# Masked softmax with given lengths: which engine loads the first four batches, and in which order

## The chip, the core and the metric

The kernel runs on one core of one Trainium2 chip. The metric is the device time of one execution in microseconds; three runs of the kernel before gave a median of 156.31 us (156.04 to 156.49). Five engines take part: SyncE (SP) issues DMAs, GpSimd (POOL) issues DMAs and does small set-up work, VectorE (DVE) and ScalarE (ACT) compute, and TensorE (PE) does two tiny matmuls. All DMAs, whoever issues them, are moved by the core's 16 DMA engines.

## The reference

The input x has 16 batches of 8 heads of 256 rows of 256 float32; each batch has a length between 128 and 255.

```python
for b in range(batch):
    length = lengths[b]
    masked = x[b, :, :, :length].copy()
    masked = masked - np.max(masked, axis=-1, keepdims=True)
    exp_masked = np.exp(masked)
    result[b, :, :, :length] = exp_masked / np.sum(exp_masked, axis=-1, keepdims=True)
```

Columns from the length on are zero in the result. The lengths of the draw used are 188, 233, 229, 243, 195, 252, 165, 210, 222, 180, 209, 157, 159, 199, 214, 248.

## The kernel before

One batch is 2048 rows: 128 partitions with 16 rows each, 2 MB. The tile xt holds 8 slots of one batch; batch n lives in slot n % 8 from its load to its store, and every step works in place.

For each batch, in order, there are these steps:

- Load. SyncE issues batches 0 to 3 whole (lines 128 to 132, batch 0 as two halves), all at the start, on its own DMA queue (q1). GpSimd issues batches 4 to 15 on another queue (q0), in a loop of six turns with two loads each (lines 177 to 184). A loaded row is only as wide as the batch needs: `pick` (line 147) compares the length with the widths 160, 168, up to 240, and 256, by nested branches, and issues the DMA with the first width that holds the length.
- Mask. VectorE's clip (line 221) takes, over columns 128 to 255, the smaller of x and a number that is very large inside the length and very negative outside it. Columns that were not loaded hold old finite data or zeros, and are masked too.
- Exponential. ScalarE (line 328) works row by row of each partition, 16 instructions a batch, and adds up the row sums.
- Divide. VectorE takes the reciprocal of the sums (line 242) and multiplies each half batch by it (line 245).
- Store. SyncE issues the stores on the same queue as its loads (lines 134 to 143), whole or cut into halves and quarters by `parts`.

VectorE's order is written out: for batch 0 and from batch 4 on, the first half's divide, then the next batch's mask, then the second half's divide; for batches 1 to 3 the next batch's mask comes first.

The order between engines is set by semaphores. Stores start only after the third half batch has been exponentiated (line 134), and a batch's stores wait until those of the batch two before have landed (line 140). s_st counts landed stores, one semaphore for even batches and one for odd ones; each is started at 64 by a small memset (line 170). Before the loop, GpSimd zeroes columns 160 to 255 of slots 4 to 7, which have never held a whole batch (line 173; four memsets), after it has waited for VectorE's set-up (line 171). Then it waits for the lengths, for these four fills, and for batch 2 to land (s_ld[3], line 176). In the loop a load waits, from the second turn on, until the load two batches before it has landed (s_sw, line 182) and until the batch that last used the slot is stored (s_st, line 183).

At the end, VectorE checks sums and lengths, and a rarely used second path (from line 290 on) would do everything again with the row maximum subtracted.

Of the kernel before, what the change touches and what calls it, by code (L numbers as in the profile page):

```python
# [9 lines left out]
F32 = mybir.dt.float32  # L10
# [7 lines left out]
POOL = mybir.EngineType.Pool  # L18
# [3 lines left out]
def kernel(  # L22
# [6 lines left out]
    nc = tc.nc  # L29
    P = nc.NUM_PARTITIONS  # L30

    batch, heads, seq_q, seq_k = x.shape
# [6 lines left out]
    x_f = x.rearrange("b h q k -> b (h q) k").rearrange("b (p t) k -> b p t k", p=P)  # L39
    out_f = out.rearrange("b h q k -> b (h q) k").rearrange("b (p t) k -> b p t k", p=P)  # L40

    slots = 8
    ahead = 4
    assert slots - ahead == 4 and batch % slots == 0

    widths = list(range(160, 248, 8))
    low = widths[0]
# [3 lines left out]
    def parts(b):  # L51


        if b == 0:
            cuts = [0, nt]
        elif b < 8:
            cuts = [0, half, half + quarter, nt]
        elif b < 13 or b == batch - 1:
            cuts = [0, half, nt]
        else:  # L60
            cuts = [0, nt]
        return [slice(i, j) for i, j in zip(cuts, cuts[1:])]

    pool = ctx.enter_context(tc.tile_pool(name="all", bufs=1))
    psum = ctx.enter_context(tc.tile_pool(name="psum", bufs=1, space=bass.MemoryType.PSUM))
    xt = pool.tile([P, slots, nt, seq_k], F32, name="xt")
    word64 = pool.tile([1, batch], mybir.dt.int64, name="word64")
    word = word64.bitcast(I32)
# [3 lines left out]
    len_s = pool.tile([P, batch], F32, name="len_s")  # L72
# [2 lines left out]
    row_sum = pool.tile([P, batch, nt], F32, name="row_sum")  # L75
    inv_sum = pool.tile([P, batch, nt], F32, name="inv_sum")
    warm = pool.tile([P, 1], F32, name="warm")
    seed = pool.tile([1, 2], F32, name="seed")

    sum_low, sum_high = 1.0e-15, 1.0e30  # L80
    ones_c = pool.tile([P, 1], BF16, name="ones_c")
# [10 lines left out]
    s_st = [sem("s_st0"), sem("s_st1")]  # L92
    with tc.tile_critical(no_gpsimd_drain=True):  # L93
# [4 lines left out]
        s_ld = [sem(f"s_ld{k}") for k in range(ahead + 1)]  # L98

        s_sw = [sem("s_sw0"), sem("s_sw1")]  # L100

        s_iota = sem("s_iota")
        s_fill = sem("s_fill")
# [14 lines left out]
        def length(engine, at):  # L118

            return nc.values_load(  # L120
                at,
                engines=[engine],
                skip_runtime_bounds_check_because="compared with constants, never an address",
            )
# [2 lines left out]
        nc.scalar.dma_start(out=word64, in_=lengths[None, :]).then_inc(s_word, 16)  # L127
        for h in range(2):
            s = slice(h * half, (h + 1) * half)
            nc.sync.dma_start(out=xt[:, 0, s], in_=x_f[0, :, s]).then_inc(s_ld[h], 16)  # L130
        for b in range(1, ahead):
            nc.sync.dma_start(out=xt[:, b], in_=x_f[b]).then_inc(s_ld[b + 1], 16)  # L132

        nc.sync.wait_ge(s_exp, 3)
        for b in range(batch):
            s_b = s_st[b % 2]
            for s in parts(b):
                nc.sync.wait_ge(s_out, 2 * b + (s.stop - 1) // half + 1)
                if b >= 2 and s.start == 0:
                    nc.sync.wait_ge(s_b, 64 * (b // 2 + 1))  # L140
                nc.sync.dma_start(
                    out=out_f[b, :, s, :], in_=xt[:, b % slots, s, :]
                ).then_inc(s_b, 16 * ((s.stop - s.start) // quarter))


# [1 line left out]
        def pick(v, n, slot, par, ws):  # L147

            if len(ws) == 1:
                w = ws[0]  # L150
                nc.gpsimd.dma_start(  # L151
                    out=xt[:, slot, :, :w], in_=x_n[:, n, :, :w]
                ).then_inc(s_sw[par], 16)
                return
            m = (len(ws) - 1) // 2
            with nc.gpsimd.If(v <= ws[m]):  # L156
                pick(v, n, slot, par, ws[: m + 1])
            with nc.gpsimd.Else():
                pick(v, n, slot, par, ws[m + 1 :])
# [6 lines left out]
        ).then_inc(s_iota, 1)  # L166
        nc.gpsimd.memset(ones, 1.0).then_inc(s_ones, 1)  # L167
        nc.gpsimd.memset(ones_c, 1.0).then_inc(s_ones, 1)
        for par in range(2):
            nc.gpsimd.memset(seed[:, par : par + 1], 0.0).then_inc(s_st[par], 64)  # L170
        nc.gpsimd.wait_ge(s_v, 2)
        for b in range(ahead, slots):
            nc.gpsimd.memset(xt[:, b, :, low:], 0.0).then_inc(s_fill, 1)  # L173
        nc.gpsimd.wait_ge(s_word, 16)
        nc.gpsimd.wait_ge(s_fill, slots - ahead)
        nc.gpsimd.wait_ge(s_ld[ahead - 1], 16)
        with nc.Fori(0, (batch - ahead) // 2, 1, engines=[POOL]) as q:
            for par in range(2):
                n = 2 * q + (ahead + par)
                v_len = length(POOL, word[0:1, bass.ds(2 * n, 1)])  # L180
                with nc.gpsimd.If(q >= 1):  # L181
                    nc.gpsimd.wait_ge(s_sw[par], 16 * q)
                    nc.gpsimd.wait_ge(s_st[par], 64 * q)
                pick(v_len, bass.ds(n, 1), bass.ds(n % slots, 1), par, widths + [seq_k])


        nc.tensor.wait_ge(s_ones, 2)
# [8 lines left out]
        def step(ins):  # L196
# [8 lines left out]
                out=down, in0=iota_i, scalar1=0.5, scalar2=-big, op0=ALU.add, op1=ALU.mult  # L205
# [7 lines left out]
                out=len_s, in0=len_f, scalar1=big, scalar2=None, op0=ALU.mult  # L213
# [4 lines left out]
        def clip(b, s, lo, hi):  # L218

            t = xt[:, b % slots, s, lo:hi]  # L220
            return nc.vector.scalar_tensor_tensor(  # L221
                out=t,
                in0=down[:, None, lo:hi].to_broadcast([P, s.stop - s.start, hi - lo]),
                scalar=len_s[:, b : b + 1],
                in1=t,
                op0=ALU.add,
                op1=ALU.min,
            )

        def mask(b, s):  # L230
            if b == 0:
                nc.vector.wait_ge(s_ld[s.start // half], 16)
            elif b < ahead:
                nc.vector.wait_ge(s_ld[b + 1], 16)
            else:
                nc.vector.wait_ge(s_sw[b % 2], 16 * ((b - ahead) // 2 + 1))
            clip(b, s, mid, seq_k).then_inc(s_min, 1)

        def divide(b, h):
            s = slice(h * half, (h + 1) * half)  # L240
            nc.vector.wait_ge(s_exp, 2 * b + h + 1)
            step(nc.vector.reciprocal(out=inv_sum[:, b, s], in_=row_sum[:, b, s]))  # L242
            nc.vector.wait_ge(s_v, v)
            t = xt[:, b % slots, s, :]
            nc.vector.tensor_tensor(  # L245
                out=t,
                in0=t,
                in1=inv_sum[:, b, s, None].to_broadcast([P, half, seq_k]),
                op=ALU.mult,
            ).then_inc(s_out, 1)  # L250

        mask(0, slice(0, half))
        mask(0, slice(half, nt))
        for b in range(batch):


            first = b == 0 or b >= ahead
            if first:
                divide(b, 0)
            if b + 1 < batch:  # L260
                mask(b + 1, slice(0, nt))
            if not first:
                divide(b, 0)
            divide(b, 1)
# [14 lines left out]
        for k, (_, _, edge, op) in enumerate(checks):  # L279
            nc.vector.tensor_scalar(  # L280
                out=bad[:, k : k + 1],
# [13 lines left out]
        with nc.vector.Else():  # L295
            with nc.Fori(0, batch, 1, engines=[DVE]) as i:
                nc.vector.wait_ge(g_ld, 16 * i + 16)
                nc.vector.scalar_tensor_tensor(
                    out=g_t,
                    in0=down[:, None, :].to_broadcast([P, nt, seq_k]),  # L300
                    scalar=len_s[:, bass.ds(i, 1)],
# [6 lines left out]
                    out=neg_max, in_=g_t, op=ALU.max, axis=AX, negate=True  # L308
# [5 lines left out]
                    out=g_t,  # L314
# [24 lines left out]
        a_redo = length(ACT, redo_bits[0:1, 0:1])  # L339
        with nc.scalar.If(a_redo >= 1):  # L340
            for par in range(2):
                nc.scalar.wait_ge(s_st[par], 64 * (batch // 2 + 1))
            with nc.Fori(0, batch, 1, engines=[ACT]) as i:
                nc.scalar.dma_start(out=g_t, in_=x_g[:, bass.ds(i, 1)]).then_inc(g_ld, 16)
                nc.scalar.wait_ge(g_v, 3 * i + 2)
                with nc.Fori(0, nt, 1, engines=[ACT]) as t:
                    e = g_t[:, bass.ds(t, 1), :]
                    nc.scalar.activation(
                        out=e,
                        in_=e,  # L350
                        func=EXP,
                        bias=neg_max[:, bass.ds(t, 1)],
                        accum_out=sum_g[:, bass.ds(t, 1)],
                    ).then_inc(g_exp, 1)
                nc.scalar.wait_ge(g_out, i + 1)
                nc.scalar.dma_start(out=o_g[:, bass.ds(i, 1)], in_=g_t).then_inc(g_st, 16)
                nc.scalar.wait_ge(g_st, 16 * i + 16)


    with tc.tile_critical(no_gpsimd_drain=True):  # L360
        for par in range(2):
            nc.sync.wait_ge(s_st[par], 64 * (batch // 2 + 1))


# [28 lines left out]
```

## Time and profile before

| | |
|---|---|
| median of 3 runs | 156.31 us (156.04 to 156.49) |
| the profiled execution | 156.38 us |
| its span, first to last instruction | 154.8 us |
| VectorE busy, ScalarE busy | 116.8 us, 105.2 us |
| GpSimd busy | 19.1 us |
| DMA moved | 62.09 MB, 401 GB/s over the span |
| read from HBM, written to HBM | 28.51 MB, 33.55 MB |
| SyncE's three whole loads: issue to landing (median) | 16.0 us |
| first load by GpSimd issued at | 20.80 us |
| first store issued at | 19.62 us |

Times inside the execution are microseconds from the start of the span. A row of the profile's views names the source line, the engine and the operation, with what it writes and what it reads; "POOLq" and "SPq" are the instruction queues of GpSimd and SyncE. The DMA share of a stretch is the mean busy share of the 16 DMA engines in it. Packets that overlap in one engine can bring it a little above 1.

### The profile page before, as it was taken

Reading aid. Unit: us, or ns where it says so; the run is one execution under the profiler, and the core shown is the slowest. Engines: PE = TensorE matmul, PEld = TensorE weight load, DVE = VectorE, ACT = ScalarE, POOL = GpSimd, SP = SyncE. Lnnn points to the kernel's source line nnn. Section 1 sums busy time; section 2 is a strip of 40 time slices with the busy share of each in tenths; the row PEclk is TensorE's granted clock in tenths of the full one; section 3 lists DMA queues with packets and bytes.
Section 4 is the critical chain, followed back from the end, with each engine's and each line's share of the span. In section 5 each row is a group of like instructions: output and inputs, shape, how many; then the busy total and the mean of one; then the engine's idle time right before and its main releaser. Section 6 shows DMA issues by size and latency. Waiting matters only on the chain.

```text
span 154.8 us, 1298 instructions
## 1 busy us (share of the span) xinstructions
PE 0.3 (0%) x2; PEld 0.2 (0%) x2; DVE 116.8 (75%) x91; ACT 105.2 (68%) x514; POOL 19.1 (12%) x26
## 2 busy tenths in 40 slices
PE   0000000000000000000000000000000000000000
PEld 0000000000000000000000000000000000000000
DVE  1349999954999696969799796969696556986800
ACT  3096799991792959597796959595959709779000
POOL 4910031000220200202020020202010000000000
DMA  4999999999999999999999999999999999999992
GB/s 112 424 443 432 436 364 406 403 414 450 407 402 389 415 414 418 414 414 413 400 421 410 415 408 406 416 415 419 418 423 412 418 455 409 426 455 419 421 421 91
DMA packets 9989, 62.09 MB, mean 401 GB/s; under 512 B 850, under 2 KB 946, under 8 KB 6274
## 3 DMA queue, kind: packets, MB, share of 16 engines
q1 hardware_dynamic: 5904, 41.95, 65.7%
q0 software_dynamic: 4080, 20.12, 32.1%
q14 instruction: 3, 0.02, 0.0%
q10 hardware_dynamic: 2, 0.00, 0.0%
HBM read 28.51 MB, written 33.55 MB: 401 GB/s over the span
## 4 chain that ended last, share of the span: by engine, by line
DMA 73%; DVE 7%; issue 6%; ACT 4%; POOLq 2%; ACTq 1%; SPq 1%; PE 0%
DMA xt<-in_x_dram 73%; ACT xt L328 4%; DVE xt L221 3%; DVE xt L245 3%; ACTq L328 1%; POOLq L156 1%; POOLq L151 1%; SPq L130 1%; DVE ends L277 0%; POOLq L120 0%; DVE inv_sum L242 0%; SPq L132 0%; DVE bad L280 0%; POOLq L181 0%; ACTq L334 0%
## 5 line engine op out<-in xcount | busy, mean ns | idle before, releaser
L328 ACT ACTIVATE xt<-xt (+1 forms) x256 | 102.4, 402 | 36.1 <-DVE xt L221 36.1
L245 DVE TENSOR_TENSOR xt<-xt,inv_sum 128x2048 f32<-128x2048 f32 x32 | 73.3, 2292 | 1.1
L328 ACT ACTIVATION_READ_ACCUMULATOR xt<-xt (+1 forms) x256 | 48.0, 187 | 0.0
L221 DVE SCALAR_TENSOR_TENSOR xt<-down,len_s,xt 128x2048 f32<-128x2048 f32 (+1 forms) x17 | 37.8, 2222 | 12.1 <-DMA xt<-in_x_dram 11.9
L151 POOL DMA_DIRECT2D xt<-in_x_dram x12 | 12.8, 1066 | 94.5 <-DMA out_dram<-xt 61.1
L242 DVE RECIPROCAL inv_sum<-row_sum 128x8 f32<-128x8 f32 x32 | 6.3, 198 | 14.3 <-ACT xt L328 14.3
L173 POOL MEMSET xt<- 128x1536 f32 x4 | 5.3, 1393 | 1.1 <-DVE len_s L212 1.1
L321 ACT ACT_TABLE_LOAD x1 | 1.3, 1283 | 1.6 <-SPq L93 1.6
L204 DVE TENSOR_SCALAR down<-iota_i 128x256 f32<-128x256 int32 x1 | 0.3, 300 | 1.6 <-POOL iota_i L164 1.6
L277 DVE TENSOR_REDUCE ends<-row_sum 128x1 f32<-128x256 f32 x2 | 0.7, 408 | 0.0
L191 PE MATMUL count<-bad,ones_c 128*1 128x3 bf16 x1 | 0.2, 165 | 143.8 <-DVE bad L280 143.8
L209 DVE CAST len_b<-word 1x16 bf16<-1x16 int32 x1 | 0.2, 163 | 0.4 <-DMA word<-in_lengths_dram 0.4
L212 DVE TENSOR_SCALAR len_s<-len_f 128x16 f32<-128x16 f32 x1 | 0.2, 175 | 0.3 <-PE len_f L189 0.3
L164 POOL IOTA iota_i<- 128x256 int32 x1 | 0.3, 332 | 0.6 <-SPq L93 0.6
L288 DVE TENSOR_REDUCE redo<-count 1x1 f32<-1x3 f32 x1 | 0.1, 149 | 0.3 <-PE count L191 0.3
L280 DVE TENSOR_SCALAR bad<-ends 128x1 bf16<-128x1 f32 x3 | 0.3, 149 | 0.0
L170 POOL MEMSET seed<- 1x1 f32 x2 | 0.2, 226 | 0.0
L191 PEld LDWEIGHTS count<-bad,ones_c 128*1 128x1 bf16 x1 | 0.1, 79 | 143.9 <-DVE bad L280 143.9
L321 ACT ACTIVATE warm<-const-float32-0.0 128x1 f32<-128x1 f32 x1 | 0.2, 203 | 0.0
L167 POOL MEMSET ones<- 1x128 bf16 x1 | 0.2, 197 | 0.0
L189 PE MATMUL len_f<-len_b,ones 1*128 1x16 bf16 x1 | 0.2, 166 | 2.6 <-DVE len_b L209 2.6
L277 DVE TENSOR_REDUCE ends<-len_s 128x1 f32<-128x16 f32 x1 | 0.2, 157 | 0.0
(7 smaller groups left out, 0.6 us busy)
## 6 DMA issues: line engine op xcount, KB each, us to landing
out_dram<-xt SPq DMA_DIRECT2D x19, 1024.0 KB
out_dram<-xt SPq DMA_DIRECT2D x14, 512.0 KB
xt<-in_x_dram SPq DMA_DIRECT2D x3, 2048.0 KB, 16.0
out_dram<-xt SPq DMA_DIRECT2D x3, 2048.0 KB
xt<-in_x_dram POOLq DMA_DIRECT2D x3, 1728.0 KB, 16.4
xt<-in_x_dram POOLq DMA_DIRECT2D x2, 2048.0 KB, 18.5
xt<-in_x_dram POOLq DMA_DIRECT2D x2, 1600.0 KB, 16.4
xt<-in_x_dram POOLq DMA_DIRECT2D x2, 1280.0 KB, 14.5
```

Source lines behind the costliest of these rows:

```text
L130: nc.sync.dma_start(out=xt[:, 0, s], in_=x_f[0, :, s]).then_inc(s_ld[h], 16)
L151: nc.gpsimd.dma_start(out=xt[:, slot, :, :w], in_=x_n[:, n, :, :w]).then_inc(s_sw[par], 16)
L156: with nc.gpsimd.If(v <= ws[m]):
L164: nc.gpsimd.iota(iota_i, pattern=[[1, seq_k]], base=0, channel_multiplier=0).then_inc(s_iota, 1)
L173: nc.gpsimd.memset(xt[:, b, :, low:], 0.0).then_inc(s_fill, 1)
L191: nc.tensor.matmul(count, lhsT=ones_c, rhs=bad, start=True, stop=True).then_inc(s_count, 1)
L221: return nc.vector.scalar_tensor_tensor(out=t, in0=down[:, None, lo:hi].to_broadcast([P, s.stop - s.start, hi - lo]), scalar=len_s[:, b : ...
L242: step(nc.vector.reciprocal(out=inv_sum[:, b, s], in_=row_sum[:, b, s]))
L245: nc.vector.tensor_tensor(out=t, in0=t, in1=inv_sum[:, b, s, None].to_broadcast([P, half, seq_k]), op=ALU.mult,).then_inc(s_out, 1)
L277: step(nc.vector.tensor_reduce(out=ends[:, k : k + 1], in_=values, op=op, axis=AX))
L321: nc.scalar.activation(out=warm, in_=nc.const_aps.tensor(0.0, (P, 1), F32), func=EXP)
L328: ins = nc.scalar.activation(out=e, in_=e, func=EXP, accum_out=sum_h[:, i, j])
```

## The change

The order of work is no longer the order of the batches. A position is mapped to a batch by `batch_of`: positions 0, 1 and 2 are batches 1, 2 and 3, position 3 is batch 0, and from 4 on they agree. SyncE loads positions 0 to 2 whole. GpSimd loads positions 3 to 15 by their length, in a loop of seven turns whose last turn has one load. Its first load (batch 0, into slot 3) is issued after one fill and the lengths, with no wait for a landing. The other four fills, and the wait for position 2's landing, stand in the first turn, between the first load and the second. The semaphores of even and odd positions change places in the loop, and the one of the odd positions is started at 128.

```diff
-    ahead = 4
+    ahead = 3
+    def batch_of(pos):
+        return pos + 1 if pos < ahead else 0 if pos == ahead else pos
...
-            nc.sync.dma_start(out=xt[:, b], in_=x_f[b]).then_inc(s_ld[b + 1], 16)
+            nc.sync.dma_start(out=xt[:, b], in_=x_f[batch_of(b)]).then_inc(s_ld[b + 1], 16)
...
-                    nc.sync.wait_ge(s_b, 64 * (b // 2 + 1))
+                    nc.sync.wait_ge(s_b, 64 * (b // 2 + 1 + b % 2))
...
-        for par in range(2):
-            nc.gpsimd.memset(seed[:, par : par + 1], 0.0).then_inc(s_st[par], 64)
+        for k, par in enumerate((0, 1, 1)):
+            nc.gpsimd.memset(seed[:, k : k + 1], 0.0).then_inc(s_st[par], 64)
+        def fill(slot):
+            nc.gpsimd.memset(xt[:, slot, :, low:], 0.0).then_inc(s_fill, 1)
         nc.gpsimd.wait_ge(s_v, 2)
-        for b in range(ahead, slots):
-            nc.gpsimd.memset(xt[:, b, :, low:], 0.0).then_inc(s_fill, 1)
+        fill(ahead)
         nc.gpsimd.wait_ge(s_word, 16)
-        nc.gpsimd.wait_ge(s_fill, slots - ahead)
-        nc.gpsimd.wait_ge(s_ld[ahead - 1], 16)
-        with nc.Fori(0, (batch - ahead) // 2, 1, engines=[POOL]) as q:
-            for par in range(2):
-                n = 2 * q + (ahead + par)
-                v_len = length(POOL, word[0:1, bass.ds(2 * n, 1)])
-                with nc.gpsimd.If(q >= 1):
-                    nc.gpsimd.wait_ge(s_sw[par], 16 * q)
-                    nc.gpsimd.wait_ge(s_st[par], 64 * q)
-                pick(v_len, bass.ds(n, 1), bass.ds(n % slots, 1), par, widths + [seq_k])
+        nc.gpsimd.wait_ge(s_fill, 1)
+        turns = (batch - ahead + 1) // 2
+        with nc.Fori(0, turns, 1, engines=[POOL]) as q:
+            b = 2 * q + (q + 7) // 8 * ahead
+            v_len = length(POOL, word[0:1, bass.ds(2 * b, 1)])
+            with nc.gpsimd.If(q >= 1):
+                nc.gpsimd.wait_ge(s_sw[0], 16 * q)
+                nc.gpsimd.wait_ge(s_st[1], 64 * q)
+            pick(v_len, bass.ds(b, 1), bass.ds((2 * q + ahead) % slots, 1), 0, widths + [seq_k])
+            with nc.gpsimd.If(q < turns - 1):
+                b = nc.s_assert_within(2 * q + (ahead + 1), ...)
+                v_len = length(POOL, word[0:1, bass.ds(2 * b, 1)])
+                with nc.gpsimd.If(q >= 1):
+                    nc.gpsimd.wait_ge(s_sw[1], 16 * q)
+                    nc.gpsimd.wait_ge(s_st[0], 64 * q)
+                with nc.gpsimd.Else():
+                    for slot in range(ahead + 1, slots):
+                        fill(slot)
+                    nc.gpsimd.wait_ge(s_fill, slots - ahead)
+                    nc.gpsimd.wait_ge(s_ld[ahead], 16)
+                pick(v_len, bass.ds(b, 1), bass.ds(b % slots, 1), 1, widths + [seq_k])
...
-            first = b == 0 or b >= ahead
+            first = b == 0 or b > ahead
```

The remaining lines of the diff write batch_of(b) where VectorE picks a batch's length and where SyncE addresses the output, and carry the new counts to the last waits. VectorE's order over positions stays as it was over batches.

More of the change, by code (lines that the diff above doesn't have):

```diff
@@ L42 @@
     slots = 8
-    ahead = 4
-    assert slots - ahead == 4 and batch % slots == 0
+    ahead = 3
+    assert ahead == 3 and slots == 8 and batch == 16
+    def batch_of(pos):
+        return pos + 1 if pos < ahead else 0 if pos == ahead else pos
     widths = list(range(160, 248, 8))
@@ L77 @@
     warm = pool.tile([P, 1], F32, name="warm")
-    seed = pool.tile([1, 2], F32, name="seed")
+    seed = pool.tile([1, 3], F32, name="seed")
     sum_low, sum_high = 1.0e-15, 1.0e30
@@ L129 @@
             s = slice(h * half, (h + 1) * half)
-            nc.sync.dma_start(out=xt[:, 0, s], in_=x_f[0, :, s]).then_inc(s_ld[h], 16)
+            nc.sync.dma_start(out=xt[:, 0, s], in_=x_f[batch_of(0), :, s]).then_inc(s_ld[h], 16)
         for b in range(1, ahead):
-            nc.sync.dma_start(out=xt[:, b], in_=x_f[b]).then_inc(s_ld[b + 1], 16)
+            nc.sync.dma_start(out=xt[:, b], in_=x_f[batch_of(b)]).then_inc(s_ld[b + 1], 16)
         nc.sync.wait_ge(s_exp, 3)
@@ L139 @@
                 if b >= 2 and s.start == 0:
-                    nc.sync.wait_ge(s_b, 64 * (b // 2 + 1))
+                    nc.sync.wait_ge(s_b, 64 * (b // 2 + 1 + b % 2))
                 nc.sync.dma_start(
-                    out=out_f[b, :, s, :], in_=xt[:, b % slots, s, :]
+                    out=out_f[batch_of(b), :, s, :], in_=xt[:, b % slots, s, :]
                 ).then_inc(s_b, 16 * ((s.stop - s.start) // quarter))
@@ new lines @@
+        turns = (batch - ahead + 1) // 2
[7 more added lines that the diff above has]
+            with nc.gpsimd.If(q < turns - 1):
+                b = nc.s_assert_within(
+                    2 * q + (ahead + 1),
+                    ahead + 1,
+                    batch - 2,
+                    skip_runtime_bounds_check_because="q < turns - 1",
+                )
+                v_len = length(POOL, word[0:1, bass.ds(2 * b, 1)])
+                with nc.gpsimd.If(q >= 1):
+                    nc.gpsimd.wait_ge(s_sw[1], 16 * q)
[6 more added lines that the diff above has]
+                pick(v_len, bass.ds(b, 1), bass.ds(b % slots, 1), 1, widths + [seq_k])
@@ L223, in clip @@
                 in0=down[:, None, lo:hi].to_broadcast([P, s.stop - s.start, hi - lo]),
-                scalar=len_s[:, b : b + 1],
+                scalar=len_s[:, batch_of(b) : batch_of(b) + 1],
                 in1=t,
@@ L235, in mask @@
             else:
-                nc.vector.wait_ge(s_sw[b % 2], 16 * ((b - ahead) // 2 + 1))
+                nc.vector.wait_ge(s_sw[(b - ahead) % 2], 16 * ((b - ahead) // 2 + 1))
             clip(b, s, mid, seq_k).then_inc(s_min, 1)
@@ L341 @@
             for par in range(2):
-                nc.scalar.wait_ge(s_st[par], 64 * (batch // 2 + 1))
+                nc.scalar.wait_ge(s_st[par], 64 * (batch // 2 + 1 + par))
             with nc.Fori(0, batch, 1, engines=[ACT]) as i:
@@ L361 @@
         for par in range(2):
-            nc.sync.wait_ge(s_st[par], 64 * (batch // 2 + 1))
+            nc.sync.wait_ge(s_st[par], 64 * (batch // 2 + 1 + par))
 _INS = ['x', 'lengths']
```

## The prediction

> **What bounds the kernel now.** I read the page's busy times first, then its DMA queues, then the same by stretches of the span.
>
> ```profile
> PE 0.3 (0%) x2; PEld 0.2 (0%) x2; DVE 116.8 (75%) x91; ACT 105.2 (68%) x514; POOL 19.1 (12%) x26
> ...
> q1 hardware_dynamic: 5904, 41.95, 65.7%
> q0 software_dynamic: 4080, 20.12, 32.1%
> ```
>
> No compute engine is above 75%. The two queues' packets took 65.7 + 32.1 = 97.8% of the 16 DMA engines' span, 151.4 of 154.8 us. q1 is SyncE's queue (whole loads, then every store), q0 GpSimd's (loads by length). The stretches (columns: stretch, length, busy time of PE, PEld, DVE, ACT, POOL, clock, DMA share, GB/s) show no hole:
>
> ```profile
> 2.00:18.00 16.00, 0.17 (x1) 0.10 (x1) 9.69 (x9) 9.34 (x43) 5.34 (x4) 1.00 0.99 409
> 18.00:20.50 2.50, 0.00 (x0) 0.00 (x0) 2.40 (x2) 2.50 (x13) 0.00 (x0) 1.00 1.01 433
> 20.50:23.70 3.20, 0.00 (x0) 0.00 (x0) 3.13 (x5) 3.20 (x17) 1.30 (x1) 1.00 1.02 348
> ...
> 42.00:131.00 89.00, 0.00 (x0) 0.00 (x0) 73.90 (x51) 65.58 (x325) 9.78 (x9) 1.00 1.02 414
> 131.00:151.50 20.50, 0.17 (x1) 0.08 (x1) 13.31 (x16) 10.01 (x50) 0.00 (x0) 1.00 1.00 426
> ```
>
> The DMA share (next to last) is 1.0 from 2 us to the end. So the time is the first packet (2.15), plus the DMA engines' work, plus 1.7 us from the last landing (153.05 in the trace's landing records) to the end of the span. A byte less is time less, if no hole opens. SyncE's queue has the same reading:
>
> ```profile
> SPq L140 <- DMA out_dram<-xt: 95.3, 14, 9.3
> SPq L138 <- DVE xt L245: 14.6, 1, 14.6
> SPq L141 <- DVE xt L245: 11.4, 8, 3.3
> ```
>
> It waits 95.3 us for older stores to land and only 11.4 us for results: finished batches queue for the DMA.
>
> **The change, part by part.** I call position p the p-th batch worked on. Now p0 to p3 are batches 0 to 3, whole, through q1. After, p0 to p2 are batches 1 to 3, whole, and p3 is batch 0 through q0. Its length in the given draw is 188, so 192 of 256 columns are read.
>
> *Bytes.* A whole batch is 8 packets of 16384 B per DMA engine; their duration in the trace is 611 ns, so 4.89 us. A narrow batch is 128 rows per engine. Rows of 184 columns went six to a packet at 178 ns (29.7 each), rows of 200 six at 190.4 ns (31.7 each). Between them, 30.7 ns for 192: 128 x 30.7 = 3.93 us. Removed: **0.96 us** of every engine's work. Loads of p4 to p15 and all stores are unchanged.
>
> *When p3's packets start.* GpSimd's timeline now:
>
> ```profile
> 3.05 5.34 POOL L173 MEMSET xt<- 128x1536 f32 x4 [1.10 <-DVE len_s L212]
> 20.80 1.30 POOL L151 DMA_DIRECT2D xt<-in_x_dram  x1 [12.41 <-issue]
> 23.96 0.56 POOL L151 DMA_DIRECT2D xt<-in_x_dram  x1 [1.86 <-issue]
> ```
>
> After, one fill (1.39 us) ends at 4.44, and the wait for batch 2's landing no longer stands ahead of the first load. From that wait's end to the load took 18.57 to 20.80 = 2.23 us; with some 0.2 for the added register steps, the load issues at 6.9. Its first packet follows late: 20.80 to 26.22 now, 5.4 us (4.7 for a later load that met an empty q0). So p3 starts at **12.3**. The other four fills (5.6 us) come behind it on GpSimd, end before 18 even if they start at 12.3, and only p4's load waits on them.
>
> *What that does to q1.* Where both queues are full, the packet records alternate one for one whatever the size: in 1 us near 34 us, 47 packets of 4800 B on q0 beside 44 of 4096 on q1; near 37 us, 22 of 16384 beside 24 of 4096. At 12.3, q1 has 0.9 us of p1 (now landed at 13.21) and the 8 packets of p2 left: 9.5 packets, each followed by one of p3 at 184 ns. p1 lands at 13.5, p2 at 18.07 + 1.75 = **19.8**.
>
> *The hand-over to stores.* The first store is issued 6.4 us after p1 lands (13.21 to 19.62), so at 19.9; an issue takes 1.0 us to its first packet (1.13 to 2.15), so 20.9. From 19.8 to 20.9 q0 works alone: p3 has 12 of its 22 packets left, 2.2 us. No row shows a narrow load alone. The nearest, a whole load on q0 beside few stores (36 to 42 us), ran at 437 GB/s; I take 0, and if narrow packets alone ran at half rate, +0.55. Work then continues to 22.1 + 4.9 (store of p0) = 27.0. The next store needs p2: 18.07 to its issue at 23.39 is 5.3, plus 1.0: 19.8 + 6.3 = 26.1, before 27.0. p4's load, issued on p2's landing, took 18.07 to 26.22 = 8.15; so at most 28.0, and stores cover until then. No hole, with 0.9 us in hand.
>
> *A start-up loss.* From 20.5 to 23.7 p3's packets were stretched (up to 1.3 us instead of 0.61; the 348 GB/s above). Against the usual durations that is 0.7 us, right when GpSimd's first load and the first store are issued; otherwise only the very first loads show it. I take it as paid once as now. Bounds: gone, -0.7; paid twice, +0.7.
>
> *The added load on q0.* The last of the 16 completion writes came 0.06 us after the 15th at the first whole load, 0.42 at 96 us, 0.82 at the end: one engine falls behind, 0.76 us over ten narrow loads. One more: +**0.08**. The Trainium skill ("DMA: Bandwidth & Descriptors", Latency and other measured facts) tells of two engines that usually run slower and suspects the software-built descriptor rings. The lag here agrees in direction.
>
> *Waits, later.* Each later load waits, as before, for the load two positions earlier and the store eight earlier; parity 0 and 1 change places and a third seed moves the counts along. SyncE issues one load fewer (0.65 us, before a wait of 14.6), GpSimd one more and a third seed memset (0.1 us, inside the 1.10 us that it waits ahead of its fills); both engines idle there. The stores keep their order. If p4 starts up to 1.8 us later, q0's loads land that much later, and stores fill the place. The tail covers it: p14's mask starts at 125.41, the last result is ready at 145.45, 20.0 us of ACT and DVE, and the last store is issued at 145.48. Alone it needs 1.0 + 2.45 us (its landing follows the one before by 2.45), plus 0.82 lag: 149.75. It lands at 153.05, so 3.3 us of cover, 2.4 after the gain.
>
> Sum: -0.96 + 0.08 = **-0.88 us**. The profiled execution took 156.38 with a span of 154.8; so 155.5 and 153.9. It lies 0.07 above the median, 156.31, from which I forecast **155.4**.
>
> **The rivals.**
> *A. Early packets (same).* If p3 began 1.0 us after its issue, as SyncE's loads do, at 7.9, q1 has 17.4 packets left (0.45 us of p0, 16 whole). p2 lands at 18.07 + 3.2 = 21.3, the next store comes at 27.6, and the DMA is dry for 0.6 us after 27.0. Time: 156.3 - 0.88 + 0.6 = 156.0. Against it: 5.4 and 4.7 us in two loads that met an empty q0. The Trainium skill (same page, Specifications) gives about 1 us to the first byte of a GpSimd load, which speaks for this rival; the two rows here are far above it.
> *B. The dry hand-over (slower).* If the queues shared by bytes, not packets, or the fills made later starts worse, p3 would finish with p2, both at 22.1. Then store of p0 ends at 27.0, the next comes at 22.1 + 6.3 = 28.4, p4 later still. Dry 1.4 us: 156.3 - 0.88 + 1.4 = 156.8. It decides from p2's landing at 20.7 (first hole) and costs more than the gain from 21.6. For it: the margin is under 1 us, and the stretched start could fall on p2. Against it: packets alternate one for one.
> *C. Hidden by the load chain (same).* p4, p6, up to p14 each wait for one another. If p4's delay grew to 3.3 us by p14, results would set the end at 153.05 and the gain be eaten: 156.3. Against it: q0 is never empty from 43 to 131 us, so only its start moves, by at most 1.8 us.
>
> **How the numbers follow.** Forecast 155.4: 0.62 (all of it faster). A 156.0: 0.12. C 156.3: 0.08. B 156.8: 0.18. About 0.3% (0.47 us) can be told from no change. So faster 0.62, same 0.20, slower 0.18. The forecast's own range is 154.7 (stretch gone) to 155.8; 0.55 and 0.7 above it lead into A and B. Over all cases I take 154.7 to 156.7, which leaves out some of B.
>
> **What would show it.** q0 grows to about 21.7 MB, q1 falls to about 39.85, read bytes fall by 0.52 MB to 27.98. p3's load issues near 6.9 and its packets start near 12.3; p2 lands near 19.8 (18.07 now); DMA share stays at 1.0 between 20 and 30 us; the last landing moves from 153.05 to about 152.2. Wrong: a DMA share clearly under 1 between 20 and 30 us (A, B), p2's landing after 20.7, p14's mask after 128 us (C), or packets of p3 far from 184 ns.

## The result and the profile after

The changed kernel takes 156.99 us (156.84 to 157.14, 6 runs) against 156.30 of the kernel before: a ratio of 1.0045, 95% interval 1.0028 to 1.0062. I had forecast 155.4, a range over all cases up to 156.7, and a chance of 0.18 for "slower"; the result lies above the range. The profiled execution took 156.96 us with a span of 155.3.

The bytes went as the diff says. The queue lines of the page after (packets, MB, share of 16 engines):

```profile
q1 hardware_dynamic: 5760, 39.85, 62.4%
q0 software_dynamic: 4448, 21.69, 35.7%
```

There are 0.52 MB less than before, but the two shares add up to 98.1% of a longer span: 152.3 us of packet time, against 151.4. Fewer bytes took more packet time, so some packets became longer. The same stretches as in the prediction show where (last two columns: DMA share, GB/s):

```profile
2.00:18.00 16.00, 0.17 (x1) 0.10 (x1) 8.25 (x9) 7.90 (x35) 8.03 (x6) 1.00 1.01 398
18.00:20.50 2.50, 0.00 (x0) 0.00 (x0) 1.91 (x1) 2.50 (x14) 0.00 (x0) 1.00 0.95 365
20.50:23.70 3.20, 0.00 (x0) 0.00 (x0) 1.63 (x1) 3.20 (x18) 0.26 (x1) 1.00 1.10 402
...
26.00:36.00 10.00, 0.00 (x0) 0.00 (x0) 9.90 (x8) 9.36 (x47) 0.56 (x1) 1.00 0.99 347
...
42.00:131.00 89.00, 0.00 (x0) 0.00 (x0) 74.79 (x53) 65.72 (x325) 9.76 (x9) 1.00 1.02 416
131.00:151.50 20.50, 0.17 (x1) 0.08 (x1) 13.31 (x16) 10.80 (x54) 0.00 (x0) 1.00 1.00 426
```

The kernel before has in the stretch that the prediction left out:

```profile
26.00:36.00 10.00, 0.00 (x0) 0.00 (x0) 6.87 (x5) 9.55 (x48) 0.00 (x0) 1.00 0.99 409
```

From 42 us on next to nothing has changed (414 and 426 before). The loss lies ahead of it: 398 GB/s from 2 to 18 us, where it was 409, and 347 from 26 to 36, where it was 409. The DMA share is 0.99 there all the same: the engines are not idle, they are slow.

GpSimd's timeline after shows the first load where it was expected, and the second one late:

```profile
7.03 1.29 POOL L156 DMA_DIRECT2D xt<-in_x_dram  x1 [2.59 <-issue]
8.32 5.36 POOL L179 MEMSET xt<- 128x1536 f32 x4
23.45 1.15 POOL L156 DMA_DIRECT2D xt<-in_x_dram  x1 [9.77 <-issue]
26.86 0.56 POOL L156 DMA_DIRECT2D xt<-in_x_dram  x1 [2.27 <-issue]
```

and SyncE's own waits moved towards computed results (after the first store, the longest wait for a result was 3.3 us, it is 5.4):

```profile
SPq L145 <- DMA out_dram<-xt: 92.3, 13, 8.8
SPq L143 <- DVE xt L271: 16.8, 1, 16.8
SPq L146 <- DVE xt L271: 15.3, 7, 5.4
```

The 5.4 us are the wait for the second store. SyncE issues the first and the second store here:

```profile
21.05 0.42 SPq L146 DMA_DIRECT2D out_dram<-xt  x1
26.89 0.38 SPq L146 DMA_DIRECT2D out_dram<-xt  x1
```

The trace's packet records give the rest of the story, position by position:

- p3's packets start at 11.6. Beside them p2's whole packets take about 660 ns from 14 us on, instead of 611. p2 lands between 19.6 (first engine) and 21.5 (last).
- From 20 to 22 us q0 works all but alone: p3's packets come to 230 ns there, and took 183 before.
- The first store's packets start at 22.1, 1.0 us after its issue, and nearly all of them have ended by 27.7. The second store is issued at 26.89; its first packet starts at 30.3, and on most engines its packets start after 31.
- From 27.5 to 31.5 p4's narrow packets are all but alone, and stretched: 226 to 364 ns on average in each half microsecond, single ones up to 1025, instead of 187.

In sums per engine (packet time of all engines over 16), after less before: bytes -0.96; p3's own packets 4.36 instead of 3.93, +0.43; the whole packets of p1 and p2, 10.26 instead of 9.78, +0.48 (0.37 of it in p2; 0.08 of it falls between 8 and 10 us, before p3's first packet); p4's packets of six rows 5.39 instead of 3.97, +1.42; and the loss that the kernel before had on its fourth load from 20.9 to 23 us, -0.58, gone. That is +0.79, against +0.71 in the mean landing of the last store (151.83 to 152.54), +0.59 on the last engine and +0.69 in the median time.

### The profile page after: what moved, and what is told of

It reads as the page before. It is cut to its first block, busy times and chain, and to the rows that moved or that the text cites. A ratio compares the mean times of both kernels' runs of the same rounds, so it can differ in the third digit from the quotient of the medians.

```text
span 155.3 us, 1340 instructions
## 1 busy us (share of the span) xinstructions
PE 0.3 (0%) x2; PEld 0.2 (0%) x2; DVE 116.8 (75%) x91; ACT 105.4 (68%) x514; POOL 21.6 (14%) x29
## 4 chain that ended last, share of the span: by engine, by line
DMA 65%; DVE 16%; ACT 5%; issue 5%; SPq 1%; ACTq 1%; POOLq 1%; PE 0%
DMA xt<-in_x_dram 44%; DMA out_dram<-xt 21%; DVE xt L271 9%; DVE xt L247 6%; ACT xt L354 5%; ACTq L354 1%; DVE inv_sum L268 1%; SPq L146 1%; SPq L135 1%; DVE ends L303 0%; POOLq L161 0%; POOLq L156 0%; SPq L137 0%; DVE bad L306 0%; ACTq L360 0%
## 5 line engine op out<-in xcount | busy, mean ns | idle before, releaser
L156 POOL DMA_DIRECT2D xt<-in_x_dram x13 | 13.9, 1071 | 92.9 <-DMA out_dram<-xt 66.4
L179 POOL MEMSET xt<- 128x1536 f32 x5 | 6.7, 1399 | 1.1 <-DVE len_s L238 1.1
```

What stands on the lines that cost most here:

```text
L156: nc.gpsimd.dma_start(out=xt[:, slot, :, :w], in_=x_n[:, n, :, :w]).then_inc(s_sw[par], 16)
L179: nc.gpsimd.memset(xt[:, slot, :, low:], 0.0).then_inc(s_fill, 1)
```

## The experiments

Before and after are the two kernels; the first kernel's median was 156.06 to 156.22 in these runs. Theory T at the start: the loss is the lack of stores beside q0's narrow packets. Rival U: it is a start-up loss that only changes its place.

**The second load without its wait.**

```diff
-                    nc.gpsimd.wait_ge(s_ld[ahead], 16)
```

> The changed kernel without GpSimd's wait for position 2's landing ahead of its second load (p4). Theory T (no cover): the loss sits where q0's narrow packets have no stores beside them: p3's last 12 packets alone (230 ns instead of 182), and p4's from 27.4 to 31.5 us (about 320 ns on average instead of 187, +1.4 us in all) because q1 has run dry. Here p4 is issued near 16 and follows p3 in q0 at 23, beside the first store; q1 is not dry before 30. T expects p4's packets near 187 ns and 157.0 - 1.4 = 155.6 us. Rival U (a start-up loss): the stretched packets of 26 to 31.5 us are the loss that the kernel before had at 20.5 to 23.7, and come once whatever lies beside: 156.9 to 157.0, with about 1 us of stretched packets somewhere between 15 and 32.

155.88 us, ratio 0.9983 (0.9973 to 0.9994): 0.2% faster than the kernel before, and about 1 us faster than after. The profiled execution was the slowest of its twelve, 156.35 us. p4 is issued at 15.03 and follows p3 in q0. The table of stretches at the hand-over, for the kernel before, after, and this one:

```profile
20.00:22.00 2.00, 0.00 (x0) 0.00 (x0) 1.97 (x3) 2.00 (x11) 1.20 (x1) 1.00 1.05 344
23.00:26.00 3.00, 0.00 (x0) 0.00 (x0) 2.97 (x4) 3.00 (x17) 0.56 (x1) 1.00 1.02 418
26.50:31.50 5.00, 0.00 (x0) 0.00 (x0) 4.93 (x5) 5.00 (x27) 0.00 (x0) 1.00 0.98 410
```

```profile
20.00:22.00 2.00, 0.00 (x0) 0.00 (x0) 0.00 (x0) 2.00 (x11) 0.00 (x0) 1.00 1.00 328
23.00:26.00 3.00, 0.00 (x0) 0.00 (x0) 2.96 (x3) 2.55 (x14) 1.15 (x1) 1.00 1.02 437
26.50:31.50 5.00, 0.00 (x0) 0.00 (x0) 4.97 (x5) 4.67 (x24) 0.56 (x1) 1.00 0.95 268
```

```profile
20.00:22.00 2.00, 0.00 (x0) 0.00 (x0) 0.20 (x1) 2.00 (x12) 0.00 (x0) 1.00 0.98 323
23.00:26.00 3.00, 0.00 (x0) 0.00 (x0) 2.97 (x3) 2.28 (x12) 0.00 (x0) 1.00 1.05 374
26.50:31.50 5.00, 0.00 (x0) 0.00 (x0) 4.97 (x4) 5.00 (x26) 0.09 (x1) 1.00 0.98 413
```

The 268 GB/s of after are 413 again, and p4's packets cost 4.50 us instead of 5.39. They are not at 187 ns, as T had it: from 22 to 25 us they run alone at an even 230, because the first store, issued at 21.34, has its first packet at 25.0. No packet of p4 is stretched like those of after (the longest takes 240 ns). This run speaks against U in the form that the loss comes once whatever is done.

**Batch 0 narrow, but on SyncE's own queue** (kernel before, changed order).

```diff
+        return (pos + 1) % ahead if pos < ahead else pos
...
-            nc.sync.dma_start(out=xt[:, b], in_=x_f[b]).then_inc(s_ld[b + 1], 16)
+            w = 192 if b == 3 else seq_k
+            nc.sync.dma_start(
+                out=xt[:, b, :, :w], in_=x_f[batch_of(b), :, :, :w]
+            ).then_inc(s_ld[b + 1], 16)
...
+        nc.gpsimd.memset(xt[:, 3, :, 192:], 0.0).then_inc(s_fill, 1)
```

> The kernel before, in the changed order of batches, with batch 0 as the fourth load of SyncE's own queue and read 192 columns wide, whatever its length (a constant in the code). Nothing runs beside it and GpSimd's loads are as before. Theory T: a narrow load alone is no cheaper than a whole one (21.3 packets of 4608 at 230 ns = 4.9 us against 8 x 0.61 = 4.9): 156.3, within 0.3 of the kernel before. The rival, by bytes (30.7 ns a row wherever it runs): 155.4.

155.70 us, ratio 0.9975 (0.9964 to 0.9986): between the two. The load goes as 2048 packets of 768 B at 36 to 41 ns on average, and lands 4.66 us after the load ahead of it, where an unstretched whole one takes 4.87. So three quarters of the bytes took 96% of the time. The rest of the gain is that the stretched packets of 20.9 to 23 us did not come: there the narrow packets keep an even 41 ns.

**Batch 0 whole, beside the others.**

```diff
-            pick(v_len, bass.ds(b, 1), bass.ds((2 * q + ahead) % slots, 1), 0, widths + [seq_k])
+            with nc.gpsimd.If(q < 1):
+                nc.gpsimd.dma_start(out=xt[:, ahead], in_=x_f[0]).then_inc(s_sw[0], 16)
+            with nc.gpsimd.Else():
+                pick(v_len, bass.ds(b, 1), bass.ds((2 * q + ahead) % slots, 1), 0, widths + [seq_k])
```

> The changed kernel with batch 0 loaded whole by GpSimd, at the same place and time. Theory T: in after p3 cost 10 x 0.18 + 12 x 0.231 + 10 x 0.05 (longer whole packets beside it) = 5.1 us, so a whole p3 (8 x 0.61 = 4.9, no longer packets beside it) costs no more; p2 lands near 23 instead of 21.5, so the dry time of q1 grows a little: 157.0 to 157.6. By bytes: 157.0 + 0.96 = 158.0 or more.

159.57 us, ratio 1.0226 (1.0213 to 1.0239), far above T and in the range of its rival, but not for the rival's reason. Whole packets beside whole ones stay at 611 ns on both queues, as T said, and the packet time of the whole run grows by only 0.4 us over after. But batch 0's packets start at 10.2, 1.4 us earlier than p3's in after, p2 lands at 23.4, the first store starts at 24.6, and the DMA share falls in between:

```profile
20.00:22.00 2.00, 0.00 (x0) 0.00 (x0) 1.97 (x3) 1.58 (x8) 0.00 (x0) 1.00 0.99 426
23.00:26.00 3.00, 0.00 (x0) 0.00 (x0) 2.09 (x1) 3.00 (x16) 0.69 (x1) 1.00 0.62 262
26.50:31.50 5.00, 0.00 (x0) 0.00 (x0) 4.96 (x4) 5.00 (x26) 0.54 (x1) 1.00 0.99 308
```

The hole is 2.0 us of all engines more than in after, and it is most of the 2.6 us lost. Sharing the DMA with another load delays p2, and with p2 all that follows. The last line shows that stretched packets are here too: at the same DMA share as elsewhere, the first store's last packets take up to 1518 ns.

**Divide first, so that the second store comes in time.**

```diff
-            first = b == 0 or b > ahead
+            first = b <= 1 or b > ahead
```

> The changed kernel with VectorE dividing position 1's first half before it masks position 2 (as it does for position 0 and from 4 on). The next store no longer waits for p2's landing: it is issued near 23.6 instead of 26.9 and queues behind the first. Theory T: q1 is not dry from 27.7 to 31.1, p4's packets run beside stores at 187 ns, 157.0 - 1.4 = 155.6. Rival U: the stretch is not undone by company: 157.0.

156.66 us, ratio 1.0046 (1.0033 to 1.0059): no gain on after, whose ratio was 1.0045. T has failed here. The second store is issued at 23.61 and q1 is full until 31.1, yet:

```profile
26.50:31.50 5.00, 0.00 (x0) 0.00 (x0) 4.97 (x4) 5.00 (x27) 0.56 (x1) 1.00 0.97 325
```

Now the store's own packets are stretched (423 and 502 ns on average from 28 to 30 us, instead of 310), and p4's later. Company alone does not undo the loss. It may follow p4's late start, which this kernel shares with after (issue at 23.44); this run does not show that.

**Second profiles of both kernels.**

> The kernel before, unchanged, for a second profile. In the first one, packets between 20.5 and 23.7 us were stretched (about 0.6 us of all engines' time in sum). If that is part of the kernel's course (theory U, a start-up loss that each kernel pays at a place of its own), it stands at the same place again, 0.4 to 0.8 us. If it is chance, it is gone or elsewhere.

> The changed kernel, unchanged, for a second profile. Theory U: the stretched packets between 26 and 32 us are there again, 1.0 to 1.6 us in sum. Chance: gone or elsewhere.

Both repeat (155.99 and 157.00 us). The kernel before stretches its fourth load from 21 to 23 us again (0.55 us in sum), the changed one p4 from 27 to 32 (5.23 us instead of 3.97). It is not chance.

**An early first store, without and with the second load's wait.**

```diff
-            cuts = [0, nt]
+            cuts = [0, half, nt]
...
-        nc.sync.wait_ge(s_exp, 3)
```

> e1_second_load_free, with SyncE's wait for the third exponential taken away and position 0's store cut in halves, so that the first store is issued near 14 us and stands in q1 behind p2's load. Theory T2: a narrow packet costs 178 to 190 ns beside a full q1 and 230 where q1 is empty, and in e1_second_load_free about 25 packets of each engine (19.8 to 25.2 us) ran beside an empty q1: 25 x 0.044 = 1.1 us. Here q1 is not empty before 30 us, so 155.9 - 1.1 = 154.8. Rival: the width of a packet's time does not matter, the DMA engines are as busy either way: 155.9.

> The changed kernel with that same early first store, GpSimd's wait for p2's landing left in. T2: only p3's last 12 packets gain (12 x 0.05 = 0.6), p4 still starts near 27.5 and the stretched packets after it stay: 157.0 - 0.6 = 156.4. Rival (what costs is the late hand-over of q1, stretch included): with the store queued in time both go, 157.0 - 0.6 - 1.3 = 155.1.

Without the wait 156.33 us, ratio 1.0008 (0.9996 to 1.0020); with it 156.45, 1.0021 (1.0007 to 1.0036). p3 gets cheaper, as T2 said: 4.16 and 4.06 us. But now the whole packets of p2, just ahead of the first store, are stretched from 17 to 20.5 us: 10.8 us for the whole loads instead of 10.25. The first run lies above T2's 154.8 and above its rival's 155.9. The second comes out at T2's 156.4, but by luck: p3 gains 0.30 and not 0.6, the whole packets cost 0.53 more, and p4's packets, which T2 left stretched, cost 4.54 instead of 5.39.

**Where the stretched packets belong.** Two runs of the kernel before, with the first store early (by the edit above) and late:

```diff
-        nc.sync.wait_ge(s_exp, 3)
+        nc.sync.wait_ge(s_exp, 4)
```

> The kernel before with the early first store of e8_early_store (no wait for the third exponential, position 0 stored in halves), nothing else. In both profiles of the kernel before, packets were stretched from 20.9 to 23 us (0.7 us), one to two us after the first store's issue; in e8_early_store, whose first store was issued at 13.6, from 17 to 20.5. Theory S: the stretch belongs to q1's first turn from loads to stores and moves with the first store; here, with the fourth whole load still ahead of the store, it stands on that load's last packets again, 20 to 23 us, and the time is that of the kernel before, 156.1 within 0.3. Rival: it belongs to the moment of the store's issue, and moves to 15 to 18.

> The kernel before with the first store held until four halves are exponentiated instead of three, so it is issued near 22.8, just before p3's load has landed. Theory S: the stretched packets follow the first store and come after 22.8, if at all. Rival: they stand at 20.9 to 23 because of something else there, GpSimd's first load (issued at 20.8) above all. Time: the store still comes before q1 is dry, or 1 us late: 156.1 to 157.

Early: 156.26 us, ratio 1.0009 (0.9997 to 1.0020), stretched from 19.5 to 23.5, on the fourth load's last packets, as S said, though the fourth load's packets now cost 1.19 us more than usual, where in the kernel before it was 0.58. The time does not show this: a sum of packet times is not yet a time. Late: 157.34, ratio 1.0068 (1.0055 to 1.0081). The late one tells most. Its lines:

```profile
20.00:22.00 2.00, 0.00 (x0) 0.00 (x0) 1.97 (x3) 2.00 (x11) 1.20 (x1) 1.00 1.05 451
23.00:26.00 3.00, 0.00 (x0) 0.00 (x0) 2.97 (x4) 3.00 (x17) 0.56 (x1) 1.00 0.98 254
```

From 20 to 22 us no packet is longer than 616 ns, with GpSimd's first load issued at 20.80 as in the kernel before: that load alone is not the cause. The store is issued at 22.80 and has its first packet at 26.7; between the two, GpSimd's first narrow load (p4) is alone and stretched: its packets of six rows cost 5.58 us instead of 3.97. This is the picture of after, made out of the kernel before by a store that is 3 us late.

**Narrow loads only after the whole ones.**

```diff
-        fill(ahead)
+        for slot in range(ahead, slots):
+            fill(slot)
...
+        nc.gpsimd.wait_ge(s_ld[ahead], 16)
         turns = (batch - ahead + 1) // 2
...
-                with nc.gpsimd.Else():
-                    for slot in range(ahead + 1, slots):
-                        fill(slot)
-                    nc.gpsimd.wait_ge(s_fill, slots - ahead)
-                    nc.gpsimd.wait_ge(s_ld[ahead], 16)
...
-            first = b == 0 or b > ahead
+            first = b <= 1 or b > ahead
```

> The changed kernel with the early first store, VectorE dividing position 1's first half before masking position 2, and GpSimd's loads moved: all fills first, then the wait for p2's landing, then p3 (batch 0 by its length) and p4 with no further wait. So whole loads run with nothing beside them, and p3 and p4 run beside stores that are already in q1. Theory T2 (a narrow packet saves only beside stores): p1 and p2 take 0.611 a packet and land at 13.2 and 18.1, p3's packets take 180 to 190 ns from 23 on, and the byte saving comes through: 156.1 - 0.9 = 155.2, if no hole opens before p3. Rival (the stretched packets at the turn grow by as much): 156.0 or more.

160.37 us, ratio 1.0269 (1.0237 to 1.0301). The test is spoiled: GpSimd issued p3 at 25.78, 6.4 us after its wait for p2 ended instead of 2.2, the DMA had nothing from 26.3 to 27.8, and the third position's store came at 42. Where p3 did run beside stores (32 to 35 us), its packets took 182 to 184 ns. But stretched packets came twice: on p2 from 15.5 us on, with no narrow load beside it (10.87 us for the whole loads instead of 9.78), and on p3's first packets from 27.8 on (5.37 us for p3 instead of 3.93). GpSimd had finished the load's address arithmetic at 21.9; why the issue came 3.8 us later is not settled.

**The second load later still.**

```diff
-                    nc.gpsimd.wait_ge(s_ld[ahead], 16)
+                    nc.gpsimd.wait_ge(s_out, 3)
```

> The changed kernel with GpSimd's second load (p4) held until position 1's first half is divided (near 26.9 us) instead of until p2 has landed, so that q0 is empty when the second store is issued. In after, that store was issued at 26.9 into an empty q1 with p4 under way in q0, and its first packets came at about 31, 4 us later; the first store, issued at 21.1 with only five of p3's packets left per engine, came after 1.1 us. Theory W (a store into an empty q1 waits behind a narrow load that is under way in q0): here its packets start 1.0 us after issue, near 28, and no packet is stretched between 26 and 31. Rival (the 4 us and the stretched packets belong to the second store itself): first packets near 31 and nothing on the DMA between 28 and 31. The time is no test: p4 comes about 5 us later than in after, more than the tail's 2 to 3 us of cover: 158 to 160.

157.32 us, ratio 1.0078 (1.0062 to 1.0095). The second store's issue and GpSimd's second load:

```profile
26.48 0.38 SPq L146 DMA_DIRECT2D out_dram<-xt  x1
```

```profile
27.87 1.15 POOL L156 DMA_DIRECT2D xt<-in_x_dram  x1 [14.19 <-issue]
```

The store's packets start at 27.3, 0.8 us after its issue, follow the first store's without a break, and none is stretched until 29.5. The next piece, issued at 28.92, behind GpSimd's load, has its first packet at 32.45, with p4's packets alone and stretched from 30.2 on. So the 4 us do not belong to the second store itself, as W said; q1 was not quite empty at its issue, though, and p4's first packet came at 30.2, 1.3 us after the next piece was issued, so W's own words fit only in part. The forecast of 158 to 160 was too high: p4 started 2.9 us later than in after, not 5.

The waits from a store's issue to its first packet, where q1 had nothing left to move before that packet, put side by side:

| store (kernel) | q0 meanwhile | issue to first packet |
|---|---|---|
| first (after) | p3's last packets, nothing behind them | 1.0 us |
| first (whole batch 0 beside) | empty | 0.8 us |
| second (after) | p4, from 0.4 us after the issue | 3.4 us |
| first (second load free) | p3's last packets, then p4 | 3.7 us |
| second (whole batch 0 beside) | p4, from 1.9 us after the issue | 3.8 us |
| first (before, late store) | p4, from the issue on | 3.9 us |
| quarter of the second (second load late) | p4, from 1.3 us after the issue | 3.5 us |

The first and the fourth row differ least: the same end of p3 is in q0, and only in the fourth is p4's load issued behind it.

## Why the prediction was wrong, step by step

- **Bytes.** Right and visible: 0.52 MB. The 0.96 us hold at the prices taken, and these were the error.
- **p3's price.** This step failed. I priced its rows from loads that ran beside stores. To take 0 for the stretch in which q0 works alone was the wrong choice: alone, six rows take 230 ns, 38.3 a row, while a whole batch's 16 rows take 611, 38.2 a row. The +0.55 that the prediction names for this and sets aside is near the +0.43 measured. Beside whole loads p3 kept 183, but made those 8% longer, which I had not thought of at all. Together 4.36 + 0.48 = 4.84 us, and a whole load costs 4.89. The saving was all but gone before the stores began.
- **Start of p3.** Forecast 12.3, measured 11.6, 4.6 us after issue. So rival A did not happen. The Trainium skill ("DMA: Bandwidth & Descriptors", Specifications) gives about 1 us for this; the trace decides. That the forecast came so near is partly luck: the same wait was 2.0 us in the kernel before with the late store, whose load is issued at 20.80 too, and 5.6 us for p4 with the divide first.
- **p2's landing.** This step failed too: 19.8 forecast, 21.5 measured. The mean engine was 2.6 us later than before, where I added 1.75; the longer packets make 0.5 of that. And the wait ends with the last engine, which came 1.9 us behind the first (0.8 before): another 0.9. p1's last engine was late as well (14.6 instead of the 13.5 forecast), and with it the first store, issued at 21.05 instead of 19.9.
- **The hand-over.** This step failed. I had 0.9 us in hand, and 1.0 us from a store's issue to its first packet. The second store was issued 5.4 us after p2's landing, as forecast, but then needed 3.4 us to its first packet and over 4 on most engines. Rival B named the place and its point (p2 after 20.7) and, with 156.8, nearly the time. Its mechanism is not the one seen, so that is luck: the DMA is hardly dry (a share of 0.95 from 26.5 to 31.5 us leaves 0.25 us where B had 1.4), it carries p4 alone, in stretched packets. That is the largest term, +1.42, and the run with the free second load takes 0.89 of it away.
- **The start-up loss.** "Paid once as now" does not describe it. The loss of the fourth load is gone with that load (-0.58), and stretched packets came on p4 instead; the two together are +0.84, a little beyond my bound of +0.7.
- **The lag of one engine.** I added 0.08, from one profile. The last engine's lag at the end was 0.82 us there, but 0.11 in the second profile of the same kernel, and 0.13 and 0.31 in the two of after. So a lag that grows with each narrow load is not shown. The Trainium skill ("DMA: Bandwidth & Descriptors", Latency and other measured facts) suspects the descriptor rings where two engines run slower; these records name no engine and can't test that.
- **The tail.** Right: p14's mask starts at 126.21, 0.8 later, and the last store is issued 0.8 later; rival C did not happen.

What stays open is why packets are stretched. Shown: they stand at the same place in repeated profiles, they come around the first stores, they moved when the first store was held back, and they hit loads, stores and narrow packets alike. In most runs they fill the two to four microseconds up to a store's first packet: 20.6 to 23.5 us in the kernel before (first packet at 22.9), 22.8 to 27.4 in the one with the late store (26.7), 17 to 21.5 with the early store in the changed kernel (20.7). Not shown: what in the issue of a store, or in a narrow load's start, does it. The run on SyncE's own queue all but escaped it, and so did the one with the free second load, whose first store waited 3.7 us all the same.

## What to carry to other kernels

Price a transfer from a row with the same company: here a narrow load was cheaper by its bytes only beside stores, and beside loads or alone it cost nearly as much as a whole one. A DMA share near 1.0 says that the engines are occupied, not that they move bytes at their usual rate (0.95 went with 268 GB/s here, 0.98 with 413); read GB/s next to it, stretch by stretch. And where a new stream delays a landing, follow the last engine's landing to everything that waits on it: here the wait of the second load on that landing was the part to take away.

## What the runs showed of the hardware that was not expected

- The two queues alternate packet by packet (97 packets of each between 14 and 19 us in after), and a narrow queue beside whole loads lengthens the other's packets from 611 to about 660 ns; beside stores of 16 KB it did not (614).
- A store whose queue has run empty waited 0.8 to 1.0 us for its first packet with no further load in the other queue, and 3.4 to 3.9 with a narrow load under way or starting there.
- The wait from a narrow load's issue to its first packet was between 2.0 and 5.6 us, in loads that found their queue empty.
- In the span of both kernels the DMA engines also carried three instruction fetches of 8192 B, 309 ns each: the first at 25.15 us before, at 10.75 after.
